# Encoder trunk: GpSimd's adding DMAs and the block sums of seven-block weights held in written order

## The chip, the cores and the metric

The kernel runs on one core of a Trainium2 chip. The metric is the device time of one execution in microseconds, median of three runs. The core has five engines with instruction streams of their own (TensorE, VectorE, ScalarE, GpSimd and SyncE, shown in profiles as PE, DVE, ACT, POOL and SP) and 16 DMA engines. SP issues most of the transfers; POOL issues a few, among them the transfers that add what they fetch to what lies at the destination.

## The reference

Two pre-norm residual layers over 512 tokens of width 1024. The even layer adds two parallel attentions, the odd layer a neighbourhood attention with a learned position bias; each is followed by an MLP, and the MLPs are what the change touches:

```python
def sq_relu_mlp(h, w_up, w_down):        # 1024 -> 4096 -> 1024
    u = jax.nn.relu(h @ w_up)
    return (u * u) @ w_down

def reference(x, norm_mix, ev_w_in, ...):
    h = x
    for layer in range(DEPTH):           # DEPTH = 2
        i = layer // 2
        hn = rmsnorm(h, norm_mix[layer])
        if layer % 2 == 0:
            h = h + hybrid_attention(hn, ev_w_in[i], ...)
        else:
            h = h + neighbourhood_attention(hn, od_w_qkv[i], od_rpb[i], od_w_out[i])
        h = h + sq_relu_mlp(rmsnorm(h, norm_ffn[layer]), ffn_w_up[layer], ffn_w_down[layer])
    return rmsnorm(h, final_norm)
```

All inputs and outputs are float32.

## The kernel before

**Products in three passes.** A float32 operand is split into a high part (`whi`, rounded by ScalarE) and a low part (`wlo`, what is left). A product is three matmuls: high with high, high with low, low with high (`mm3`, L603 to L605).

**Three kinds of weight chunks.** `chunk` loads weights, ScalarE makes the high part (L233) and VectorE subtracts for the low part (L223). `summed_chunk` is for the eight-bank product `product8`: ScalarE writes minus the rounded weights into `wlo` (L255), then POOL issues a DMA that fetches the weights once more and adds them to that (L256); ScalarE makes the high part later (L259). `seven_chunk` is for products after Winograd's variant of Strassen's scheme (seven block products in place of eight): SP loads two blocks of rows (L352), POOL makes four block sums in three instructions (L355 to L357), then ScalarE and VectorE split the seven blocks (L361, L362), and 21 matmuls of 256 columns use them (L447 to L449).

**An MLP.** `first_product` does some of the up projection plainly and the rest in `Seven`; the sums of its activations, in `Seven.sums` (L389, L392, L395), are made by POOL. The down projection has a plain part, then `product8` (eight banks of PSUM at once), and then `Seven` over the rest, 32 chunks of weights in the first MLP. Beside `product8` VectorE and ScalarE turn the remaining activations into sums and parts (`convert`, L389 and L392, L416, L417, L421). In the first MLP alone, SP also writes the bias table of the neighbourhood attention to DRAM at this time (`bias_rows`, 48 small stores `bx<-a`, L1487 to L1493). The last conversions write into slots of SBUF that the bias rows occupy until those stores have been made. After `product8`, VectorE adds its banks to the residual (L1535).

**Order.** `weights(i)` asks for chunk `i`; `begin` and `preload` start later chunks. Outside `fixed_order()` blocks a scheduler orders each engine's instructions by priority and by when it believes them to be ready, so an instruction may stand on its engine earlier or later than it was written. `tc.keep_in_program_order(x)` holds `x` where it was written among the instructions of its engine. Every engine then runs its stream strictly in order. Weight buffers rotate: four of `raw`, three of `whi`, four of `wlo`; `seven_chunk` uses a spare activation slot (`a`) for its weights where enough are free.

Of the kernel before, what the change touches and what calls it, by code (L numbers as in the profile page):

```python
# [12 lines left out]
ALU = mybir.AluOpType  # L13
# [5 lines left out]
P = 128  # L19
# [11 lines left out]
def f32(ap):  # L31
    return ap.bitcast(F32)
# [3 lines left out]
def encoder_kernel(ctx: ExitStack, tc: tile.TileContext, ins, out, dbg=None):  # L36
    nc = tc.nc
    PE, ACT, DVE, POOL, SP = nc.tensor, nc.scalar, nc.vector, nc.gpsimd, nc.sync
# [22 lines left out]
    def nm(s):  # L61
        cnt[0] += 1
        return f"{s}_{cnt[0]}"
# [183 lines left out]
    def summed_chunk(parts, nk, ncol, heads=None, eng=None):  # L247

        raw = wp.tile([P, 1024], F32, tag="raw", bufs=4, name=nm("raw"))
        v = lambda t: t.rearrange("p (k n) -> p k n", k=nk)  # L250
        (o, n, src), = parts
        SP.dma_start(v(raw), src)
        yield
        lo_ = wp.tile([P, 1024], F32R, tag="wlo", bufs=4, name=nm("wlo"))
        ACT.activation(lo_, raw, AF.Copy, scale=-1.0)  # L255
        POOL.dma_start(v(lo_), src, accum_op=ALU.add)  # L256
        yield
        hi = wp.tile([P, 1024], F32R, tag="whi", name=nm("whi"))
        ACT.activation(hi, raw, AF.Copy)  # L259
        yield v(hi), v(lo_), []  # L260

    def rows(w, k0, nk):
        return w[k0 * P : (k0 + nk) * P, :].rearrange("(k p) n -> p k n", p=P)
# [16 lines left out]
    def begin(i):  # L280
        while begun[0] < len(loaded):
            make = asked[begun[0]][0]
            if make is summed_chunk and begun[0] > i + SUM:
                break
            if make in (summed_chunk, seven_chunk):
                next(loaded[begun[0]])
            begun[0] += 1
# [59 lines left out]
    def seven_chunk(w, k0, c0):  # L347


        slot = Slot(F32) if len(free) > reserve[0] else None  # L350
        raw = slot.t if slot else wp.tile([P, 1024], F32, tag="raw", bufs=4, name=nm("raw"))
        SP.dma_start(raw[:, 0:512].rearrange("p (k n) -> p k n", k=2), rows(w, k0, 2)[:, :, c0 : c0 + 256])  # L352
        r = raw.rearrange("p (b n) -> p b n", n=P)
        yield
        POOL.tensor_tensor(r[:, 6], r[:, 0], r[:, 1], op=ALU.subtract)  # L355
        POOL.tensor_tensor(r[:, 4:6], r[:, 2:3].to_broadcast([P, 2, P]), r[:, 0:7:6], op=ALU.add)  # L356
        POOL.tensor_tensor(r[:, 7], r[:, 3], r[:, 5], op=ALU.subtract)  # L357
        yield
        hi = wp.tile([P, 1024], F32R, tag="whi", name=nm("whi"))
        lo = wp.tile([P, 1024], F32R, tag="wlo", bufs=4, name=nm("wlo"))  # L360
        ACT.activation(hi[:, 0:896], raw[:, 128:1024], AF.Copy)  # L361
        DVE.tensor_tensor(lo[:, 0:896], raw[:, 128:1024], f32(hi[:, 0:896]), op=ALU.subtract)  # L362
        if slot:
            slot.free()
        yield hi, lo, []

    class Seven:
# [63 lines left out]
        def plan(self, w, c0, pairs=None):  # L431

            return [plan(w, pairs[kp] if pairs else 2 * kp, c0, make=seven_chunk) for kp in range(self.np)]
# [86 lines left out]
    def product8(w, first, U, evac, eng=None):  # L520


        nk = len(U)
        ids = [plan([(0, D, rows(w, k, 1))], 1, D, None, eng, make=chunk if n < 2 else summed_chunk)
               for n, k in enumerate(first)]

# [1544 lines left out]
```

## Time and profile before

| | |
|---|---|
| median of the runs | 1172.97 us (1172.79 to 1174.08, 3 runs) |
| profiled execution, device time | 1172.19 us |
| its span in the trace | 1170.3 us |
| TensorE busy | 1149.5 us (98%) |
| VectorE, ScalarE, GpSimd busy | 894.0, 668.4, 597.6 us |
| DMA: bytes, mean rate | 134.37 MB, 115 GB/s |

Of the profiled time, 1.9 us lie outside the span. The first MLP's `product8` runs from about 451 to 507 us, its seven-block product from there to about 587 us; the second MLP's `product8` begins at about 1023 us. A row of a timeline gives start, length, engine, line, operation and tile; in brackets stands how long the engine had been idle and what ended that. A row of the chain of waits gives start, length and the engine or transfer that the end of the run goes back to. A row of waits gives the total, the number and the longest. In "DMA share", 1.00 means that all 16 DMA engines are busy.

### The profile page before, as it was taken

The numbers are of one execution on the slowest core, as the hardware profiler recorded it, in microseconds if no ns is written. First come the engines' busy times: TensorE is split into PE (matmuls) and PEld (weight loads), VectorE is DVE, ScalarE is ACT, GpSimd is POOL, SyncE is SP. The second block draws the span as 40 slices with busy tenths as digits, with TensorE's granted clock in tenths as the row PEclk, the third lists the DMA queues.
The fourth block names the chain that finished last, engine by engine and source line by source line (L and its number), as shares of the span: only waits on it lengthen the run. The fifth ranks groups of instructions, "written<-read, shape, count | busy, mean of one in ns | idle before, by whom it ended". The sixth has DMA issues, their size and how long they took to land.

```text
span 1170.3 us, 20576 instructions
## 1 busy us (share of the span) xinstructions
PE 1149.5 (98%) x7348; PEld 1024.3 (88%) x7348; DVE 894.0 (76%) x1544; ACT 668.4 (57%) x1135; POOL 597.6 (51%) x744
## 2 busy tenths in 40 slices
PE   9999999999999999799999999999999999999997
PEld 7787888887899998599987988988888999989996
DVE  7887988888968876677595676767997787698765
ACT  6676876756256658433453555655552666773445
POOL 4456252305788981179802232222377799435960
PEclk9999999999999999899999999999999999999999
DMA  7322314222522327723346564434343233272332
GB/s 233 108 76 67 94 61 130 64 86 98 159 80 84 103 72 194 198 89 98 128 127 158 136 175 132 128 102 135 100 137 115 83 99 100 61 189 76 126 119 72
DMA packets 115478, 134.37 MB, mean 115 GB/s; under 512 B 9667, under 2 KB 96880, under 8 KB 115376
## 3 DMA queue, kind: packets, MB, share of 16 engines
q1 hardware_dynamic: 111024, 120.09, 33.8%
q0 software_dynamic: 4032, 12.60, 5.4%
q8 instruction: 58, 0.95, 0.3%
q10 hardware_dynamic: 320, 0.36, 0.1%
q14 instruction: 44, 0.36, 0.1%
HBM read 110.61 MB, written 6.29 MB: 100 GB/s over the span
## 4 chain that ended last, share of the span: by engine, by line
PE 79%; DVE 6%; POOL 5%; DMA 3%; issue 3%; SPq 2%; ACT 2%; DVEq 0%; POOLq 0%; ACTq 0%
PE mm L603 8%; PE mm L604 8%; PE mm L605 8%; PE s L1127 3%; PE mm L449 3%; PE mm L447 3%; PE mm L448 3%; PE o L1115 3%; PE t L1102 2%; PE t L447 2%; PE t L449 2%; PE t L448 2%; PE s L605 2%; POOL raw L357 2%; PE s L603 2%
## 5 line engine op out<-in xcount | busy, mean ns | idle before, releaser
L603 PE MATMUL mm<-a,whi 128*128 128x512 f32 x428 | 173.9, 407 | 0.2
L362 DVE TENSOR_TENSOR wlo<-a,whi 128x896 fp32r<-128x896 f32 x103 | 128.1, 1247 | 54.6 <-ACT whi L361 54.3
L604 PE MATMUL mm<-a,whi 128*128 128x512 f32 x428 | 168.9, 395 | 0.0
L605 PE MATMUL mm<-a,wlo 128*128 128x512 f32 x428 | 168.9, 396 | 0.0
L361 ACT ACTIVATE whi<-a 128x896 fp32r<-128x896 f32 x103 | 97.8, 949 | 105.3 <-PE o L604 27.5
L233 ACT ACTIVATE whi<-raw 128x1024 fp32r<-128x1024 f32 (+3 forms) x100 | 92.2, 924 | 68.1 <-PE s L604 19.4
L223 DVE TENSOR_TENSOR wlo<-raw,whi 128x1024 fp32r<-128x1024 f32 (+4 forms) x97 | 110.6, 1145 | 24.1 <-ACT whi L233 19.7
L449 PE MATMUL mm<-a,wlo 128*128 128x256 f32 x430 | 120.5, 280 | 1.0 <-DVE wlo L362 1.0
L447 PE MATMUL mm<-a,whi 128*128 128x256 f32 x430 | 120.7, 281 | 0.0
L448 PE MATMUL mm<-a,whi 128*128 128x256 f32 x430 | 120.4, 280 | 0.0
L362 DVE TENSOR_TENSOR wlo<-raw,whi 128x896 fp32r<-128x896 f32 x61 | 73.2, 1203 | 49.7 <-ACT whi L361 49.3
L361 ACT ACTIVATE whi<-raw 128x896 fp32r<-128x896 f32 x61 | 57.9, 953 | 86.4 <-POOL raw L357 54.5
L356 POOL TENSOR_TENSOR a<-a 128x256 f32<-128x256 f32 x103 | 98.6, 957 | 8.0
L355 POOL TENSOR_TENSOR a<-a 128x128 f32<-128x128 f32 x103 | 60.2, 584 | 81.6 <-DMA a<-in_ffn_w_up_dram 75.7
L357 POOL TENSOR_TENSOR a<-a 128x128 f32<-128x128 f32 x103 | 96.5, 937 | 8.0
L605 PEld LDWEIGHTS mm<-a,wlo 128*128 128x128 f32 x428 | 80.3, 188 | 18.4
L603 PEld LDWEIGHTS mm<-a,whi 128*128 128x128 f32 x428 | 80.4, 188 | 17.1 <-issue 1.3
L604 PEld LDWEIGHTS mm<-a,whi 128*128 128x128 f32 x428 | 80.7, 189 | 14.9 <-DVE a L960 0.2
L1714 POOL TENSOR_SCALAR p<-p,ti 128x256 f32<-128x256 f32 x64 | 35.4, 563 | 105.5 <-DVE ti L1713 92.3
L1135 POOL TENSOR_SCALAR p<-p,ti 128x512 f32<-128x512 f32 x64 | 45.4, 710 | 82.9 <-DVE ti L1134 55.1
L447 PE MATMUL t<-a,whi 128*128 128x256 f32 x312 | 87.6, 281 | 0.0
L448 PE MATMUL t<-a,whi 128*128 128x256 f32 x312 | 87.4, 280 | 0.0
(430 smaller groups left out, 3615.6 us busy)
## 6 DMA issues: line engine op xcount, KB each, us to landing
a<-in_ffn_w_up_dram SPq DMA_DIRECT2D x102, 256.0 KB
raw<-in_ffn_w_down_dram SPq DMA_DIRECT2D x34, 512.0 KB
raw<-in_ffn_w_down_dram SPq DMA_DIRECT2D x59, 256.0 KB
raw<-in_od_w_qkv_dram SPq DMA_DIRECT2D x64, 128.0 KB
raw<-in_ffn_w_up_dram SPq DMA_DIRECT2D x12, 512.0 KB
wlo<-in_ffn_w_down_dram POOLq DMA_DIRECT2D x12, 512.0 KB, 7.0
a<-a SPq DMA_DIRECT2D x18, 256.0 KB
bias<-bx SPq DMA_DIRECT2D x16, 256.0 KB
```

Source lines behind the costliest of these rows:

```text
L223: z = lambda: (eng or DVE).tensor_tensor(to, src, f32(high), op=ALU.subtract)
L233: ACT.activation(hi[:, 0:m], raw[:, 0:m], AF.Copy)
L356: POOL.tensor_tensor(r[:, 4:6], r[:, 2:3].to_broadcast([P, 2, P]), r[:, 0:7:6], op=ALU.add)
L357: POOL.tensor_tensor(r[:, 7], r[:, 3], r[:, 5], op=ALU.subtract)
L361: ACT.activation(hi[:, 0:896], raw[:, 128:1024], AF.Copy)
L362: DVE.tensor_tensor(lo[:, 0:896], raw[:, 128:1024], f32(hi[:, 0:896]), op=ALU.subtract)
L447: PE.matmul(o, wh, x[:, 0], start=kp == 0 and n in (0, 1, 3, 5), stop=False, skip_group_check=True)
L448: PE.matmul(o, wh, x[:, 1], start=False, stop=False, skip_group_check=True)
L449: PE.matmul(o, wl, x[:, 0], start=False, stop=kp == self.np - 1, skip_group_check=True)
L603: PE.matmul(o, wh, xh, start=first, stop=False)
L604: PE.matmul(o, wh, xl, start=False, stop=False)
L605: PE.matmul(o, wl, xh, start=False, stop=last)
```

## The change

Two places are wrapped in `tc.keep_in_program_order`: the adding DMA of `summed_chunk`, and the three block sums of `seven_chunk`. No instruction is added, removed or altered, and the orders of PE, DVE, ACT and SP stay as they were; only POOL's order moves. From L355 on, line numbers of the new kernel are one higher.

```diff
@@ summed_chunk
-        POOL.dma_start(v(lo_), src, accum_op=ALU.add)
+        tc.keep_in_program_order(POOL.dma_start(v(lo_), src, accum_op=ALU.add))
@@ seven_chunk
-        POOL.tensor_tensor(r[:, 6], r[:, 0], r[:, 1], op=ALU.subtract)
-        POOL.tensor_tensor(r[:, 4:6], r[:, 2:3].to_broadcast([P, 2, P]), r[:, 0:7:6], op=ALU.add)
-        POOL.tensor_tensor(r[:, 7], r[:, 3], r[:, 5], op=ALU.subtract)
+        held = tc.keep_in_program_order
+        held(POOL.tensor_tensor(r[:, 6], r[:, 0], r[:, 1], op=ALU.subtract))
+        held(POOL.tensor_tensor(r[:, 4:6], r[:, 2:3].to_broadcast([P, 2, P]), r[:, 0:7:6], op=ALU.add))
+        held(POOL.tensor_tensor(r[:, 7], r[:, 3], r[:, 5], op=ALU.subtract))
```

POOL's stream in the first MLP, beside `product8`, before. `wlo_5602` and `wlo_5666` are the low parts of the last two chunks of `product8`; `raw_5600`, `raw_5664` are the weights of the first two chunks of the seven-block product behind it:

```order
L256 DMA wlo_5444<-in_ffn_w_down_dram 128x1024
L256 DMA wlo_5536<-in_ffn_w_down_dram 128x1024
L355 TENSOR_TENSOR raw_5600<-raw_5600 128x128
L356 TENSOR_TENSOR raw_5600<-raw_5600 128x256
L357 TENSOR_TENSOR raw_5600<-raw_5600 128x128
L256 DMA wlo_5602<-in_ffn_w_down_dram 128x1024
L256 DMA wlo_5666<-in_ffn_w_down_dram 128x1024
L355 TENSOR_TENSOR raw_5664<-raw_5664 128x128
```

and now:

```order
L256 DMA wlo_5444<-in_ffn_w_down_dram 128x1024
L256 DMA wlo_5536<-in_ffn_w_down_dram 128x1024
L256 DMA wlo_5602<-in_ffn_w_down_dram 128x1024
L256 DMA wlo_5666<-in_ffn_w_down_dram 128x1024
L356 TENSOR_TENSOR raw_5600<-raw_5600 128x128
L357 TENSOR_TENSOR raw_5600<-raw_5600 128x256
L358 TENSOR_TENSOR raw_5600<-raw_5600 128x128
L356 TENSOR_TENSOR raw_5664<-raw_5664 128x128
```

The two adding DMAs no longer stand behind the first chunk's sums; those sums stand behind both DMAs.

POOL's stream in the second MLP at the same stage, before. `wlo_12000` and `wlo_12046` are again the last two low parts, `raw_11998` and `raw_12044` the first two seven-block chunks; `a_12234` is the sixth, loaded into a spare slot:

```order
L355 TENSOR_TENSOR raw_11998<-raw_11998 128x128
L356 TENSOR_TENSOR raw_11998<-raw_11998 128x256
L357 TENSOR_TENSOR raw_11998<-raw_11998 128x128
L256 DMA wlo_12000<-in_ffn_w_down_dram 128x1024
L355 TENSOR_TENSOR raw_12044<-raw_12044 128x128
L356 TENSOR_TENSOR raw_12044<-raw_12044 128x256
L357 TENSOR_TENSOR raw_12044<-raw_12044 128x128
L256 DMA wlo_12046<-in_ffn_w_down_dram 128x1024
L355 TENSOR_TENSOR raw_12097<-raw_12097 128x128
L355 TENSOR_TENSOR a_12234<-a_12234 128x128
```

and now:

```order
L256 DMA wlo_12000<-in_ffn_w_down_dram 128x1024
L256 DMA wlo_12046<-in_ffn_w_down_dram 128x1024
L356 TENSOR_TENSOR raw_11998<-raw_11998 128x128
L357 TENSOR_TENSOR raw_11998<-raw_11998 128x256
L358 TENSOR_TENSOR raw_11998<-raw_11998 128x128
L356 TENSOR_TENSOR raw_12044<-raw_12044 128x128
L357 TENSOR_TENSOR raw_12044<-raw_12044 128x256
L358 TENSOR_TENSOR raw_12044<-raw_12044 128x128
L356 TENSOR_TENSOR raw_12097<-raw_12097 128x128
```

Here too both DMAs go ahead of the sums, and the sums of `a_12234`, which were interleaved with those of `raw_12097`, go behind two further chunks, to the place after `raw_12161`.

In the up projections the sums move as well. At the start of the first MLP, POOL's stream before; `a_3491` is the second seven-block chunk of weights, and L389 to L395 on `a_3203`, `a_3200` are the first of four sets of activation sums:

```order
L355 TENSOR_TENSOR a_3491<-a_3491 128x128
L356 TENSOR_TENSOR a_3491<-a_3491 128x256
L357 TENSOR_TENSOR a_3491<-a_3491 128x128
L389 TENSOR_TENSOR a_3203<-a_3200 128x512
L392 TENSOR_TENSOR a_3200<-a_3200,a_3203 128x256
L395 TENSOR_TENSOR a_3203<-a_3200 128x256
```

and now, behind the fourth set:

```order
L390 TENSOR_TENSOR a_3334<-a_3331 128x512
L393 TENSOR_TENSOR a_3331<-a_3331,a_3334 128x256
L396 TENSOR_TENSOR a_3334<-a_3331 128x256
L356 TENSOR_TENSOR a_3445<-a_3445 128x128
L357 TENSOR_TENSOR a_3445<-a_3445 128x256
L358 TENSOR_TENSOR a_3445<-a_3445 128x128
L356 TENSOR_TENSOR a_3491<-a_3491 128x128
L357 TENSOR_TENSOR a_3491<-a_3491 128x256
L358 TENSOR_TENSOR a_3491<-a_3491 128x128
```

The first two chunks' sums (`a_3445` stood among the softmax rows of the attention before) come after the activations'. In the same stage one chunk that is loaded early and used late (`raw_5143`) is now summed shortly before its use, and two neighbours (`a_3796`, `a_3826`) change places. The second MLP's up projection changes in the same way.

## The prediction

> **What bounds the kernel now.** I read the chain of waits by engine first, then who TensorE waits for, then the place where it waits.
>
> ```profile
> PE 79%; DVE 6%; POOL 5%; DMA 3%; issue 3%; SPq 2%; ACT 2%; DVEq 0%; POOLq 0%; ACTq 0%
> PE s L605 <- DMA wlo<-in_ffn_w_down_dram: 7.8, 2, 6.1
> PE mm L449 <- DVE wlo L362: 1.0, 1, 1.0
> ```
>
> The first row is the chain, the others TensorE's waits (us, times, longest). TensorE ends the run; of all it waits for, the adding DMAs of `wlo` are the only large item, and the next is 1.0 us. So I look at the timelines of PE, POOL and ACT around that wait, at the end of the first MLP's `product8`.
>
> ```profile
> 484.22 0.39 PE L604 MATMUL s<-p,whi 128*128 128x512 f32 x1
> 490.74 0.79 PE L605 MATMUL s<-p,wlo 128*128 128x512 f32 x1 [6.14 <-DMA wlo<-in_ffn_w_down_dram]
> ...
> 506.44 0.39 PE L605 MATMUL s<-p,wlo 128*128 128x512 f32 x1
> 463.53 0.86 POOL L256 DMA_DIRECT2D wlo<-in_ffn_w_down_dram  x1 [13.83 <-ACT wlo L255]
> 465.52 0.86 POOL L256 DMA_DIRECT2D wlo<-in_ffn_w_down_dram  x1 [1.13 <-DMA bx<-a]
> 481.06 0.45 POOL L355 TENSOR_TENSOR raw<-raw 128x128 f32<-128x128 f32 x1 [14.69 <-ACT a L416]
> 483.22 1.77 POOL L256 DMA_DIRECT2D wlo<-in_ffn_w_down_dram  x2
> 469.06 1.04 ACT L255 ACTIVATE wlo<-raw 128x1024 fp32r<-128x1024 f32 x1
> 476.78 1.06 ACT L255 ACTIVATE wlo<-raw 128x1024 fp32r<-128x1024 f32 x1 [1.77 <-DMA raw<-in_ffn_w_down_dram]
> ```
>
> POOL stood 14.69 us before the sums of `raw_5600`, whose load SP issues late, and the last two adding DMAs stood behind them until 483.22. Their inputs were ready at 469.06 + 1.04 = 470.1 and 476.78 + 1.06 = 477.8 us.
>
> The wait also halved TensorE's clock:
>
> ```profile
> 484.00:494.00 10.00, 2.25 (x6) 1.01 (x4) 2.72 (x6) 0.49 (x1) 0.98 (x2) 0.78 0.96 198
> 488.00:490.00 2.00, 0.00 (x0) 0.00 (x0) 0.00 (x0) 0.00 (x0) 0.00 (x0) 0.90 0.87 161
> 498.00:500.00 2.00, 2.00 (x6) 1.54 (x6) 2.00 (x3) 0.53 (x1) 1.92 (x3) 0.54 0.01 2
> 472.00:484.00 12.00, 12.00 (x54) 9.77 (x53) 9.22 (x16) 6.71 (x11) 2.78 (x5) 1.00 0.61 186
> ```
>
> The last three columns are granted clock, DMA share and GB/s. A mean of 0.90 over 488 to 490 means half speed from 489.6, and 0.54 over 498 to 500 means full speed again from 499.8. TensorE's last matmul had ended at 484.61, 5.0 us before the drop.
>
> But the stall is not what the end goes back to. Here the chain of waits runs past it:
>
> ```profile
> 467.49 9.85 DMA bx<-a
> 485.36 9.56 DMA bx<-a
> 497.87 1.26 DVE wlo L362
> 507.13 1.07 DVE wlo L362
> 508.22 2.62 DMA raw<-in_ffn_w_down_dram
> 510.98 1.35 POOL raw L355
> 569.01 0.96 ACT whi L361
> ```
>
> It follows the stores of the bias table on SP to the last one, which lands at 485.36 + 9.56 = 494.92; then VectorE's work, which could not go on until that store left its slot; the low part of seven-block chunk 1 at 507.13 + 1.07 = 508.20, which frees a buffer; a load of 2.62 us; and then POOL's sums, back to back until 569.
>
> **The change part by part.**
>
> *The two adding DMAs, first MLP.* They can now go out at 470.1 and at about 478 to 480 (the load for the second shares the DMA engines, which I give up to 2 us). The first pair's tempo is the nearest for landing: the pair issued at 483.22 let TensorE start at 490.74, 7.5 us. So 470.1 + 7.5 = 478 and 478 to 480 + 7.5 = 485.5 to 487.5, against 484.61: no wait for the first, 0 to 3 us for the second, 1 taken. TensorE's naive gain is the 7.8 us of waits and half of the 499.8 - 490.7 = 9.1 us at half clock, 4.5, less 1: 11.3 us. `product8` (48 matmuls in its last phase, 46 left after 484.22, each 0.23 us as the last rows show: 506.44 ends it) would end at about 496 rather than 507.
>
> *What is late next.* The seven-block product then waits for chunk 1, ready at 508.20, less what the chain moves. Before, TensorE came to it at 506.7 + 2.5 = 509.2, after it was ready. If the chain did not move, TensorE would merely stand there instead. So the gain is the shift of the last store's landing, and no more.
>
> *How far that shift goes.* A load on quiet queues takes 2.62 us; SP issues a store every 0.61 us when nothing holds it:
>
> ```profile
> 484.75 0.57 SPq L1491 DMA_DIRECT2D bx<-a  x1
> 466.59 0.85 SPq L252 DMA_DIRECT2D raw<-in_ffn_w_down_dram  x1
> 467.49 1.09 SPq L1487 DMA_DIRECT2D bx<-a  x1
> ...
> 476.74 0.38 SPq L352 DMA_DIRECT2D raw<-in_ffn_w_down_dram  x1
> q0 software_dynamic: 288, 1.05, 53.4%
> ```
>
> With nothing beside it the last store would be out at 485.36 + 0.61 and land 2.62 later, at 488.6: 6.3 us is the upper bound. The two DMAs are moved, not removed. The last row (POOL's queue in 483 to 495) says they take 0.534 x 12 = 6.4 us of all 16 engines; between 472 and 484 those stand idle for (1 - 0.61) x 12 = 4.7 us. If the spare time is all used, 6.4 - 4.7 = 1.7 us remains to push the stores, and the shift is 6.3 - 1.7 = 4.6 us. The other estimate is from what the earlier pair did to SP: seven stores from 467.49 to 476.74 took 9.25 us where 7 x 0.61 = 4.3 would do, so 4.9 us were lost. Lost once more, the last store lands at 488.6 + 4.9 = 493.5: 1.4 us. I take the mean, 3.0 us.
>
> The Trainium skill (DMA: Bandwidth & Descriptors, Queues, rings and completion order) says that each DMA engine takes turns between queues packet by packet. By that rule the stores fall behind wherever an adding transfer runs, and the shift would be nearer the smaller estimate, 1.4 us; the long landings at 467.49 and 485.36, both beside such a pair, agree with it.
>
> *Sums of the first down chunk.* `raw_5600` now waits for the DMA of `wlo_5666` (out by 481): its sums go at 481.06 to 481.9, long before VectorE uses them at 497.87. Nothing is lost, and with that DMA 3 us later still nothing.
>
> *Up projections.* The first two chunks' sums go behind the activations'. They fill a gap:
>
> ```profile
> 283.21 1.07 POOL L395 TENSOR_TENSOR a<-a 128x256 f32<-128x256 f32 x1
> 290.38 0.47 POOL L355 TENSOR_TENSOR a<-a 128x128 f32<-128x128 f32 x1 [6.09 <-DMA a<-in_ffn_w_up_dram]
> 310.53 0.95 ACT L361 ACTIVATE whi<-a 128x896 fp32r<-128x896 f32 x1 [4.51 <-PE o L604]
> 429.30 0.46 POOL L355 TENSOR_TENSOR a<-a 128x128 f32<-128x128 f32 x1
> 431.81 0.46 POOL L355 TENSOR_TENSOR a<-a 128x128 f32<-128x128 f32 x1
> 438.93 0.94 ACT L361 ACTIVATE whi<-raw 128x896 fp32r<-128x896 f32 x1
> 443.48 0.94 ACT L361 ACTIVATE whi<-a 128x896 fp32r<-128x896 f32 x1
> ```
>
> Two chunks of 431.81 - 429.30 = 2.5 us each fit into 6.09 us of idleness, and the first is needed at 310.53, over 20 us later. `raw_5143` now comes in before the last two chunks; they end at worst 2.5 us later, at 437, and are used from 438.93 on, the last at 443.48. 0 us, at worst 1 if that cover is gone.
>
> *Second MLP.* Here TensorE had no such wait, so earlier DMAs give nothing.
>
> ```profile
> 1050.58 0.88 POOL L256 DMA_DIRECT2D wlo<-in_ffn_w_down_dram  x1
> 1059.41 0.94 ACT L361 ACTIVATE whi<-raw 128x896 fp32r<-128x896 f32 x1
> 1071.54 1.36 POOL L355 TENSOR_TENSOR raw<-raw 128x128 f32<-128x128 f32 x1 [5.01 <-DMA raw<-in_ffn_w_down_dram]
> 1074.80 0.95 ACT L361 ACTIVATE whi<-a 128x896 fp32r<-128x896 f32 x1 [1.46 <-PE o L448]
> ```
>
> Even if the last DMA went no earlier than 1050.58 + 0.88, the first two chunks' sums behind it end at 1051.5 + 5.0 = 1056.5, before 1059.41; `a_12234` fits into the 5.01 us before 1071.54 and is used at 1074.80. 0 us.
>
> *Sum.* The profiled execution took 1172.19 us (span 1170.3 and 1.9 around it), 0.78 below the median. 1172.19 - 3.0 = 1169.2; on the median, 1172.97 - 3.0 = **1170.0 us**. Behind 510.98 loads, POOL and TensorE move with the chain, so I let the 3.0 us reach the end; a measurement of this kernel tells about 0.2% (2.3 us) from no change.
>
> **The rivals.**
>
> *A new stall halves the clock (same; 25%).* TensorE comes to the seven-block product about 10 us early and stands before chunks 0 and 1. VectorE makes their low parts 507.13 - 497.87 = 9.3 us apart; less 2.5 us of matmuls for chunk 0, up to 6.8 us are idle, broken by two matmuls once chunk 1's high part is there. The drop came 5.0 us after the last matmul, and half speed then cost 4.5 us. By then TensorE is 509.2 - 505.2 = 4 us ahead, so it would come out level, and only what TensorE later waits for falls away: about 1 us, 1172.0. Against it: the two matmuls break the gap into some 3 and 4 us.
>
> The Trainium skill (TensorE: Matmul & The Clock Gate, HAM oscillation — how this bites in real kernels) puts the limit at gaps above about 3.4 us, and its Part 1 lets the clock come back after about as long a time of work; by that the broken gap could halve the clock too, at an estimated 3.4 / 2 = 1.7 us. The trace differs on the second: TensorE worked 9.1 us at half speed. On the first no gap of that length decides here.
>
> *Hidden (same; 10%).* The stores land as late as before, shift 0 to 2 us: 1172.0.
>
> *The whole stall comes back (faster; 6%).* The stores are so much quicker that the low part of chunk 1 no longer holds TensorE: 1172.97 - 11.3 = 1161.7. It would take a shift beyond the bound of 6.3.
>
> *The stores are pushed further back (slower; 17%).* All of SP's stores from 470 on now run beside two adding DMAs in place of none. Lost time on SP decides: above 6.3 us the last store lands after 494.92. If each of the two costs what the earlier pair cost together, 9.8 us are lost; the landing is 488.6 + 9.8 = 498.4, 3.5 us late, and TensorE, idle for over 10 us, restarts at half clock: 1172.97 + 3.5 = 1176.5 us, up to 4.5 more. For it: in the earlier pair's time one store took 9.85 us. Against it: that pair ran beside the load issued at 466.59 as well.
>
> That the DMAs would not move is ruled out by POOL's order; that they wait for something else on POOL belongs to the hidden case.
>
> **How the numbers follow.** The forecast (shift of 2.4 to 6.3 us) has 42%, the rivals 25, 10, 6 and 17. Faster: 42 + 6 = 48%; same: 35%; slower: 17%. The range ends at 1166.0, just under 1172.97 - 6.3 = 1166.7, and at 1176.5, so that the 6% below and about 8% of the slower case are left out. The forecast's own range is 1166.7 to 1170.6.
>
> **What would show it.** In the changed profile: L256 on POOL at about 470 and 479; no wait of 6 us for L605 there; the last `bx` store landing near 492; a wait of TensorE before L447 to L449 in its place, near 500 to 505; POOL's sums going back to back from about 508 rather than 511; the rest of the run moved by the same amount. A last store at 495 or later, or a granted clock of 0.50 beyond 505, would make the prediction wrong.

## The result, and the profile after

| | before | after |
|---|---|---|
| median (runs) | 1173.05 us (12) | 1171.74 us (12; 1170.06 to 1173.27) |
| ratio, 95% interval | | 0.9989, 0.998 to 0.9998 |
| the same pair, measured again | 1173.33 us (15) | 1171.65 us (11): 0.9985, 0.9974 to 0.9996 |
| profiled execution (span) | 1172.19 us (1170.3) | 1171.35 us (1169.6) |

The change gains 1.3 us at the first measurement (0.2 to 2.3 by the interval) and 1.7 at the second. The forecast was 1170.0, a gain of 3.0.

The chain of waits by engine, and whom TensorE waits for (us in all, times, longest), after:

```profile
PE 75%; DVE 7%; POOL 5%; DMA 4%; issue 4%; ACT 2%; SPq 2%; DVEq 0%; POOLq 0%; ACTq 0%
```

```profile
PE s L448 <- DVE hT L1536: 2.4, 1, 2.4
PE s L606 <- DMA wlo<-in_ffn_w_down_dram: 1.4, 1, 1.4
PE s L450 <- DVE wlo L363: 1.4, 3, 0.8
PE mm L450 <- DVE wlo L363: 1.2, 2, 1.1
PE t L448 <- DVE hT L1536: 1.2, 2, 0.6
```

The 7.8 us of waits for the adding DMAs have become 1.4. In their place stands a wait that the kernel before did not have: the first matmuls of the seven-block product wait for VectorE's residual adds (L1536). TensorE's timeline at that place:

```profile
487.92 0.50 PE L606 MATMUL s<-p,wlo 128*128 128x512 f32 x1 [1.43 <-DMA wlo<-in_ffn_w_down_dram]
497.57 0.39 PE L606 MATMUL s<-p,wlo 128*128 128x512 f32 x1
500.39 0.36 PE L448 MATMUL s<-a,whi 128*128 128x256 f32 x1 [2.43 <-DVE hT L1536]
501.57 0.38 PE L448 MATMUL t<-a,whi 128*128 128x256 f32 x1 [0.58 <-DVE hT L1536]
503.38 0.58 PE L448 MATMUL t<-a,whi 128*128 128x256 f32 x1 [0.60 <-DVE hT L1536]
```

`product8` ends at 498 instead of 507 us. Its banks of PSUM (`s`, `t`, `o`) are the ones that the seven-block product writes next, and each is free only when VectorE has added it to the residual. Busy time by engine in windows (the last three columns are granted clock, DMA share, GB/s) shows what that costs:

```profile
498.00:500.00 2.00, 0.00 (x0) 0.00 (x0) 2.00 (x4) 0.00 (x0) 1.84 (x4) 1.00 0.29 77
502.00:504.00 2.00, 1.40 (x8) 1.11 (x7) 2.00 (x3) 2.00 (x3) 1.84 (x4) 0.53 0.00 0
506.00:508.00 2.00, 1.87 (x9) 1.58 (x8) 2.00 (x4) 0.95 (x1) 0.00 (x0) 0.50 0.00 0
```

From 498 to 500 TensorE does nothing while VectorE (third figure) is busy throughout; from 502 to 508 TensorE runs at half clock. VectorE is late because it and ScalarE stood for the stores (the experiments below take that wait away). The rows of POOL, SP, ACT, DVE and POOL again, in order of time:

```profile
471.74 0.86 POOL L256 DMA_DIRECT2D wlo<-in_ffn_w_down_dram  x1 [4.02 <-ACT wlo L255]
480.99 0.86 POOL L256 DMA_DIRECT2D wlo<-in_ffn_w_down_dram  x1 [8.39 <-DMA bx<-a]
490.71 0.57 SPq L1494 DMA_DIRECT2D bx<-a  x1
493.29 0.63 ACT L417 ACTIVATE a<-sc 128x512 fp32r<-128x512 f32 x1 [6.75 <-DMA bx<-a]
499.57 0.67 DVE L1536 TENSOR_TENSOR hT<-hT,s 128x512 f32<-128x512 f32 x1
506.11 1.08 DVE L363 TENSOR_TENSOR wlo<-raw,whi 128x896 fp32r<-128x896 f32 x1
510.07 1.25 POOL L356 TENSOR_TENSOR raw<-raw 128x128 f32<-128x128 f32 x1 [5.35 <-DVE wlo L363]
```

The adding DMAs go out at 471.74 and 480.99. SP's last store is issued 5.35 us later than before (490.71, before 485.36); those transfers now run beside the stores. The landings behind it are short: the first of ScalarE's conversions that write into the stores' slots starts at 493.29, and SP, which waits for all the stores before it loads the table, goes on at 494.08. The same two rows before, and then SP's row after:

```profile
494.27 0.63 ACT L416 ACTIVATE a<-sc 128x512 fp32r<-128x512 f32 x1 [9.78 <-DMA bx<-a]
495.04 0.89 SPq L1788 DMA_DIRECT2D bias<-bx  x2
```

```profile
494.08 0.88 SPq L1789 DMA_DIRECT2D bias<-bx  x2
```

So the stores are out of the way 1.0 us earlier. The low part of chunk 1 is ready at 507.19 instead of 508.20, and POOL's sums go back to back from 510.07 instead of 510.98. In this pair of traces the span is 0.7 us shorter.

TensorE's own position is the clearest measure. The next table gives, for each trace of this study but the two of the failed try, how much later (+) or earlier (-) the same matmul starts than in the first trace of the kernel before: the median over the matmuls within 3 us of the time named (times as in that first trace). The kernels are those of the experiments below; "pins" are the added `keep_in_program_order`, "rows" those of the bias table.

| us, at | 362 | 410 | 440 | 540 | 930 | 1080 |
|---|---|---|---|---|---|---|
| before, second trace | 0.34 | 0.66 | 0.66 | -0.41 | 0.41 | 1.03 |
| pins in the up projections | 1.00 | 1.78 | 1.78 | 0.96 | 0.90 | 3.54 |
| after | 0.29 | 1.20 | 1.20 | -1.28 | -1.25 | -0.76 |
| after, second trace | 0.61 | 1.47 | 1.47 | -3.20 | -2.85 | -0.46 |
| pins in the down projections | 0.64 | 0.90 | 0.90 | -3.69 | -3.32 | -3.12 |
| pins in the first down projection | 0.07 | 0.32 | 0.32 | -2.97 | -2.95 | -1.12 |
| rows in own tiles, after | 0.24 | 1.21 | 1.32 | -3.87 | -4.92 | -3.67 |
| rows in own tiles, before | -0.26 | -0.23 | -0.12 | -0.43 | -1.47 | -0.58 |
| rows in own tiles, pins in the down projections | 0.14 | 0.19 | 0.29 | -6.78 | -7.34 | -6.77 |
| rows beside the seven-block product | -0.05 | 0.77 | 0.87 | -9.81 | -10.17 | -7.94 |

In the changed kernel TensorE loses 0.9 us between 362 and 410 us, in the first up projection, and gains 2.5 us between 440 and 540 us. The loss sits at two matmuls that wait for a low part of seven-block weights; the larger, before and after:

```profile
396.46 0.39 PE L449 MATMUL s<-a,wlo 128*128 128x256 f32 x1 [0.16 <-DVE wlo L362]
```

```profile
397.67 0.38 PE L450 MATMUL s<-a,wlo 128*128 128x256 f32 x1 [0.76 <-DVE wlo L363]
```

### The profile page after: what moved, and what is told of

It reads as the page before. It is cut to its first block, busy times and chain, and to the rows that moved or that the text cites. A ratio compares the mean times of both kernels' runs of the same rounds, so it can differ in the third digit from the quotient of the medians.

```text
span 1169.6 us, 20581 instructions
## 1 busy us (share of the span) xinstructions
PE 1150.6 (98%) x7348; PEld 1025.9 (88%) x7348; DVE 892.6 (76%) x1544; ACT 668.4 (57%) x1135; POOL 602.0 (51%) x744
## 4 chain that ended last, share of the span: by engine, by line
PE 75%; DVE 7%; POOL 5%; DMA 4%; issue 4%; ACT 2%; SPq 2%; DVEq 0%; POOLq 0%; ACTq 0%
PE mm L604 8%; PE mm L605 8%; PE mm L606 8%; PE s L1128 3%; PE mm L450 3%; PE mm L448 3%; PE mm L449 3%; PE o L1116 3%; PE t L1103 2%; PE s L606 2%; PE s L604 2%; POOL raw L358 2%; PE s L605 2%; PE t L448 2%; PE t L450 2%
## 5 line engine op out<-in xcount | busy, mean ns | idle before, releaser
L358 POOL TENSOR_TENSOR a<-a 128x128 f32<-128x128 f32 x103 | 98.5, 956 | 8.1
L357 POOL TENSOR_TENSOR a<-a 128x256 f32<-128x256 f32 x103 | 94.9, 921 | 8.1
L450 PE MATMUL t<-a,wlo 128*128 128x256 f32 x312 | 88.0, 282 | 0.0
```

Source lines behind the costliest of these rows:

```text
L357: held(POOL.tensor_tensor(r[:, 4:6], r[:, 2:3].to_broadcast([P, 2, P]), r[:, 0:7:6], op=ALU.add))
L358: held(POOL.tensor_tensor(r[:, 7], r[:, 3], r[:, 5], op=ALU.subtract))
L450: PE.matmul(o, wl, x[:, 0], start=False, stop=kp == self.np - 1, skip_group_check=True)
```

## The experiments

My theory after the two traces (A): the two adding DMAs bring a gain, bounded by the landing of the last store; the block sums in the up projections lose part of it. Rivals: the loss in the up projection is scatter (B); VectorE has that much work left whatever the stores do (C).

**Which pins do what.** Pinning the adding DMAs alone leaves all five streams as they were before; pinning the sums alone makes all of the change. So the split is by projection, with the sums:

```diff
-        held = tc.keep_in_program_order
+        held = tc.keep_in_program_order if w.shape[0] > D else lambda z: z
```

> The pins act in the down projections alone: the up projections' streams are those of the kernel before, the down projections' those of the changed one. Theory A (the traces' difference is real: the pins won about 2.5 us in the first down projection and lost about 1.2 us in the first up projection): TensorE runs level with the kernel before, within 0.3 us, until 440 us, is about 2.5 us ahead behind the first MLP's product8, and the time is 1170.0 to 1170.8, over 1 us below the changed kernel. Rival B (the 1.2 us lost in the up projection are the scatter of one execution): the time is that of the changed kernel, 1171.7, and the up projection may be late here too.

With the condition reversed (`== D`) and no pin on the DMAs:

> The pins act in the up projections alone; the first product8 has the stream of the kernel before. Theory A: TensorE is late by 0.9 to 1.3 us at 440 us, stands 6 and 1.7 us for the adding DMAs as in the kernel before, and the time is 1174.0 to 1174.5. Rival B: the time is that of the kernel before, 1173.0, and TensorE is level with it at 440 us.

Down projections alone: 1171.65 us against 1173.0, ratio 0.9986 (0.9977 to 0.9994). Up projections alone: 1173.74, ratio 1.0 (0.9991 to 1.0008). So the gain comes from the down projections. That the up projections' pins cost something is not seen in the times; the place in the trace shows it, with 0.8 us lost between 362 and 410 us (0.9 in the changed kernel), and 0.3 us where they are absent. TensorE stands for the adding DMAs as before:

```profile
491.59 0.80 PE L606 MATMUL s<-p,wlo 128*128 128x512 f32 x1 [5.21 <-DMA wlo<-in_ffn_w_down_dram]
495.13 0.80 PE L606 MATMUL s<-p,wlo 128*128 128x512 f32 x1 [1.89 <-DMA wlo<-in_ffn_w_down_dram]
```

Theory A's time for the down projections alone, over 1 us below the changed kernel, did not come, and for the up projections alone the time lies between the two theories'.

**The two DMAs alone.** The smallest form of the change, with the pins tied to one set of weights:

```diff
+            pinned[0] = w                      # in mlp, for l == 0, w = ffn_w_down[0]
-        held = tc.keep_in_program_order
+        held = tc.keep_in_program_order if w is pinned[0] else lambda z: z
```

> The block sums pinned in the first MLP's down projection alone: against the kernel before, GpSimd's stream differs only in the two adding DMAs that go ahead of the first chunk's three sums. Theory A (the whole gain comes from these two DMAs, the rest of the change gives nothing or loses): the same as the kernel with both down projections pinned, 1170.5 to 1172 against 1173.0 to 1173.7 for the kernel before; in the trace TensorE is level with the kernel before at 440 us within 0.4 us and 2 to 4.5 us ahead of it at 540 us. Rival: the second MLP's new order takes part, and this kernel gains under 0.5 us.

1172.09 against 1173.69 us: ratio 0.9986 (0.9977 to 0.9994), the same as with both down projections. Moving two DMAs ahead of three sums is worth 1.6 us, between 0.7 and 2.7; no gain of the rest of the change is seen beside that.

**Fewer stores beside `product8`, a failed try.** Sixteen of the 48 stores write a constant; here they go out before the first MLP from a scratch tile:

```diff
+    def neg_rows():                              # called before the first stage of the first MLP
+        t = scratch()
+        POOL.memset(t[:, 0:128], NEG)
+        ...  SP.dma_start(bxv[1, c][:, :, 128 - 128 * v : 256 - 128 * v], t[:, 0:128])
-            SP.dma_start(bxv[1, c][:, :, 128 - 128 * v : 256 - 128 * v], Fe.t[:, 256:384])
```

> The changed kernel with the 16 stores that fill the masked halves of the bias table (a constant) issued from a small constant tile before the first MLP, so that 32 of SP's 48 stores are left beside product8. Theory A (the stores set when VectorE and then TensorE go on): the last store is issued some 16 x 0.61 = 9.8 us earlier, near 481, VectorE's idle 4.5 us before its last conversions go, TensorE no longer waits for banks of the residual adds, and the time falls by 3 to 6 us below the changed kernel, 1166 to 1169. Rival C (VectorE's own queue of conversions and adds is the limit, stores or not): the time stays within 1.5 us of the changed kernel, 1170.2 or more, and TensorE waits for the residual adds as long as before (2.4 us).

> The kernel before, without pins, with the same 16 constant stores issued early. The scheduler, left free, puts one adding DMA behind the sums of the first seven-block chunk and one behind those of the second. Theory A (the early stores free the end of product8, and then the wait for the adding DMAs decides): TensorE still stands 3 to 9 us for the adding DMAs and the time is 2 to 6 us above that of the changed kernel with early constants. Rival D (with the stores out of the way POOL's order no longer matters): the two are within 1 us of each other.

Both came out slower: 1178.49 us, ratio 1.0039 (1.0026 to 1.0051), and 1175.98, ratio 1.0025 (1.0015 to 1.0035). No theory had that. TensorE's largest wait, and the chain of waits, in the first of the two:

```profile
PE s L604 <- ACT whi L259: 5.3, 2, 3.4
```

```profile
474.23 6.86 DMA bx<-a
481.34 0.70 ACT a L417 x2
482.04 0.95 ACT whi L259
```

The last store is issued at 474.23, earlier than I expected. But ScalarE's order is another: conversions into the slots now stand ahead of high parts that TensorE needs, presumably since the scheduler expects the slots free earlier, too. ScalarE then stands for the store until 481, and TensorE with it. The run says that the stores hold whatever stands behind them; as ScalarE's order moved with it, it doesn't say what fewer stores are worth.

**No conversion waits for the stores.** The rows are stored from the tile `rb`, idle at that time, and a small new one, instead of two slots. The stores keep their number and place, for which those of the constant are held:

```diff
-        R, Fi, Fe = Slot(F32), Slot(F32), Slot(F32)
+        R, Fi, Fe = Slot(F32), keep([P, S], F32, "rb"), keep([P, 376], F32, "rows_e")
...
-            SP.dma_start(bxv[1, c][:, :, 128 - 128 * v : 256 - 128 * v], Fe.t[:, 256:384])
+            held(SP.dma_start(bxv[1, c][:, :, 128 - 128 * v : 256 - 128 * v], Fe[:, 248:376]))
```

> The changed kernel, but the bias table's rows are stored from tiles of their own (one idle tile and one small new one) instead of two of the slots that the last conversions write into, so that no conversion has to wait for SP's stores; the stores themselves, their number and their place among SP's transfers stay. Theory A (the landing of the last store holds VectorE, and VectorE holds TensorE and GpSimd's sums): VectorE's idle time of 4.5 us and ScalarE's of 6.8 us before 494 us go, GpSimd's sums go back to back some 3 to 5 us earlier, TensorE's wait for the residual adds falls below 1 us, and the time is 1166 to 1169, 3 to 5 us below the changed kernel. Rival C (VectorE has that much left to do anyway): the time stays within 1.5 us of the changed kernel, 1170.2 or more.

> The kernel before with the same tiles of their own for the bias rows; GpSimd's order around the adding DMAs is that of the kernel before (two of them behind the first chunk's sums). Theory A: TensorE still stands 6 to 8 us for the adding DMAs and halves its clock, so the gain is at most what TensorE waited for behind it (about 1 us): 1172 to 1173.5; the pins are then worth 4 to 6 us rather than 1.3. Rival C: both kernels stay where they were, the pins worth 1 to 2 us.

1167.76 us with the pins, ratio 0.9949 (0.9934 to 0.9964) to the kernel before at 1173.74; 1172.12 without, ratio 0.9987 (0.9979 to 0.9995). The pins are now worth 4.4 us. Theory A's times came in both, and C falls. (Besides the tiles, a few of ScalarE's conversions and high parts, one of SP's transfers and GpSimd's filling of the rows stand in other places than before; for ScalarE and SP these are the same with pins and without, and VectorE's order is that of the kernel before, so the 4.4 us are the pins' own; what the tiles alone bring can't be told apart from these moves.) With pins, TensorE no longer waits for the residual adds; VectorE starts the first at 494.95 instead of 499.57, and the fifth at 499.96:

```profile
494.95 0.68 DVE L1536 TENSOR_TENSOR hT<-hT,s 128x512 f32<-128x512 f32 x1
499.96 0.68 DVE L1536 TENSOR_TENSOR hT<-hT,mm 128x512 f32<-128x512 f32 x1
```

What remains is the adding DMA itself, with pins and without:

```profile
489.96 0.79 PE L606 MATMUL s<-p,wlo 128*128 128x512 f32 x1 [3.06 <-DMA wlo<-in_ffn_w_down_dram]
```

```profile
490.34 0.80 PE L605 MATMUL s<-p,wlo 128*128 128x512 f32 x1 [5.71 <-DMA wlo<-in_ffn_w_down_dram]
493.92 0.79 PE L605 MATMUL s<-p,wlo 128*128 128x512 f32 x1 [1.93 <-DMA wlo<-in_ffn_w_down_dram]
```

**The faster versions.** First the same tiles with pins in the down projections alone; then, in addition, the stores beside the seven-block product instead of `product8`:

```diff
+                if i < 15: next(bias, None)      # beside product8: the loads and the first store
-            next(bias, None)
-            next(bias, None)
...
             for i, _ in enumerate(u7.run(ids[m], evac)):
                 beside(m, i)
+                if i % 3 == 2: next(bias, None)
```

> The changed kernel with tiles of their own for the bias rows and the block sums pinned in the down projections alone. If the up projection's pins cost about 1 us in each MLP, as two traces with them and two without show, this is 0.7 to 2 us below the kernel with all pins and the same tiles, 1165 to 1168, and the fastest of all; if those losses are scatter, it is level with it.

> As the kernel with tiles of their own for the bias rows and pins in the down projections, but 47 of SP's 48 stores go beside the seven-block product instead of beside product8 (all in written order). Theory A (the stores and the adding DMAs delay each other): with no stores beside them the last adding DMA lands in time, TensorE's remaining wait for it (2.5 us) and the half clock behind it (about 3 us at half speed, 1.5 us lost) go, and the time is 1162.5 to 1164.5, 1.5 to 3 us below that kernel's 1165.8. Rival: the adding DMA is slow by itself, or the stores now hold the loads of the seven-block weights behind them on SP: the same time or up to 3 us more.

1165.82 us, ratio 0.9943 (0.9926 to 0.996), 1.9 us below the same tiles with all pins by the medians and 0.7 by the ratios, with intervals that overlap, so it isn't shown which of its two forecasts came; and 1163.09 us against 1173.69, ratio 0.9908 (0.9893 to 0.9923), 10.6 us below the kernel before. In the second, TensorE's waits hold neither the adding DMAs nor the residual adds:

```profile
PE s L450 <- DVE wlo L363: 2.4, 4, 1.2
PE o L157 <- POOL zeros L130: 1.0, 1, 1.0
```

Busy time by engine in windows of the same kernel (TensorE first, granted clock third from the end):

```profile
484.00:494.00 10.00, 10.00 (x46) 8.29 (x45) 9.86 (x17) 3.38 (x7) 3.07 (x5) 1.00 0.09 28
494.00:502.00 8.00, 7.87 (x55) 7.07 (x55) 8.00 (x12) 3.80 (x5) 2.61 (x4) 1.00 0.17 51
```

It is busy almost throughout at full clock, and between 440 and 540 us it gains 10.7 us. Beside `product8` the adding DMAs now land sooner; their number, size and median time from issue to landing between 440 and 500 us, with the stores beside them (pins in the down projections, own tiles) and without:

```profile
wlo<-in_ffn_w_down_dram POOLq DMA_DIRECT2D x6, 512.0 KB, 8.1
```

```profile
wlo<-in_ffn_w_down_dram POOLq DMA_DIRECT2D x6, 512.0 KB, 6.2
```

So theory A came, in time and in mechanism. What the stores' new place is worth without the pins was not measured.

**Second traces.**

> The changed kernel once more, for a second trace and more times. If what the first trace showed is steady: TensorE loses 0.8 to 1.0 us between 362 and 410 us (up projection, pins), gains 2.5 to 4.5 us between 440 and 540, the loss in the second up projection is anything from 0.2 to 2.6, and the time is 1.0 to 1.8 us below that of the kernel before. If the up projection's loss was scatter it is under 0.4 us here.

> The kernel before once more, for a second trace. If the first trace was a lucky execution in the second MLP's up projection, as the ten other traces suggest (0.2 to 2.6 us lost there against it, 1.3 on average), this one loses 0.5 to 2.5 us there; between 440 and 540 us it is level with the first trace within 0.8 us. If instead the second up projection is slower for the pins alone, it is level there.

After: 1171.65 us, ratio 0.9985 (0.9974 to 0.9996); before, one run, 1173.17. The table has both. The loss between 362 and 410 us is 0.91, 0.86 and 0.78 us in the three traces with these pins and the up projection otherwise unchanged, and 0.32, 0.26 and 0.25 in the three further traces without them, beside 0 in the first: on average 0.6 us more, and steady, so B falls there; that this reaches the end isn't shown. (In other versions it is 0.8 us without these pins, with the rows beside the seven-block product, and 0.1 us with them, with the early constants; so it hangs on more than the pins.) In the second MLP, between 930 and 1080 us, the loss is 0.49, 2.39 and 2.64 us with the pins, 0.62, 0.20 and 1.83 without: 1.2 us more on average, but within scatter.

## Why the prediction was right and where it was wrong

The measured 1171.7 lies in the stated range, 1166.0 to 1176.5, but outside the forecast's own, 1166.7 to 1170.6. The chain that bounds the gain was named rightly, and GpSimd's sums moved by 2.5 us on average (0.9 in the first trace) where 3.0 was forecast. The time gained is less, 1.3 to 1.7 us, and that it comes out nearest to two rivals, at 1172.0, is in good part chance.

- *The adding DMAs.* Forecast for about 470 and 479 us; less TensorE's 1.2 us of delay, they went at 470.5 and 479.8. The wait for the second, 0 to 3 us with 1 taken, was 1.43 in the first trace. The naive gain of 11.3 us is about what TensorE gained where nothing took it back (10.7 us, rows beside the seven-block product).
- *What is late next.* The cause was right, VectorE's work behind the last store, but not the first instruction: TensorE met the banks that the residual adds still held, at 500.39, before it came to chunk 1. Then it came to chunk 1 just in time, as forecast: its first matmul with that low part starts at 507.25, 0.06 us after the part is ready (507.19), and as close behind it in the three other traces with these two DMAs early and the rows in slots. In the kernel before it started 1.2 us after that part was ready.
- *The clock.* I counted it against the rival that two matmuls break the gap. Gaps of 2.43, 0.58 and 0.60 us halved the clock all the same, for 6.8 us, and it halved at this place in the three other traces with these two DMAs early and the rows in slots. Half speed lasted until 508.95, beyond the 505 us that I had named as a sign of being wrong. Against its position at 440 us TensorE's lead over the kernel before fell from 10.0 us (at the matmul that starts there at 499.8) to 2.5 (at 510.5). But the half clock did not set the time. The seven-block product ends with a wait for a low part, before and after:

```profile
575.14 0.38 PE L449 MATMUL mm<-a,wlo 128*128 128x256 f32 x1 [0.95 <-DVE wlo L362]
```

```profile
574.12 0.38 PE L450 MATMUL mm<-a,wlo 128*128 128x256 f32 x1 [1.06 <-DVE wlo L363]
```

In all seven traces with the rows in slots (the failed try's apart) this matmul starts 64.05 to 64.29 us after the first of GpSimd's back-to-back sums (510.98 and 510.07 here), with 0.95 to 1.06 us of waiting before it. So the sums decide when TensorE gets through, as forecast, and what the half clock cost TensorE it would otherwise have waited. The rival's half clock came; that the time is near its 1172.0 is not its doing.

- *The shift of the stores, 3.0 us.* Its parts held: the stores were pushed back, and the gain stayed far below the stall. Where SP goes on behind the stores, the four traces with the two DMAs early and rows in slots have 494.08, 493.23, 492.34 and 492.81 against 495.04 and 495.00 in the two of before: a shift of 0.9 to 2.7 us, 1.9 on average. That is nearer to the smaller of my two estimates, 1.4 us, which the Trainium skill's rule favoured (DMA: Bandwidth & Descriptors, Queues, rings and completion order: turns packet by packet), and the first trace alone would belong to the rival "hidden". GpSimd's sums go back to back at 510.07, 508.45, 507.55 and 508.02 against 510.98 and 511.04, 2.5 us earlier on average; why by more than the stores isn't settled. Between 440 and 540 us TensorE gains 2.48, 4.67, 4.59 and 3.29 us in the four traces, 3.8 on average, against 0, 1.07 and 0.82 in the three without: a difference of 3.1 us. (These gains hold what TensorE had lost up to 440 us and got back, as the sums decide.)
- *"0 us, at worst 1 if that cover is gone" for the up projections* is a step that failed by size: 0.6 us in the first. I had checked the first chunks and the last, not the ones between: GpSimd's sums run almost back to back there, and a new order among them shows up as waits for low parts at 367 and 397 us (the second is there without the pins too, but shorter).
- *"I let the 3.0 us reach the end"* is the other. With only the two DMAs moved, the time falls by 1.6 us (0.7 to 2.7), half of the 3.1 in the traces. Part of it is that traces are single executions: the first of before is 0.86 us below its kernel's median, and the second ends 1.1 us later in span; that of the pins in the down projections is the fastest of its 11 runs, and that of the pins in the up projections the slowest of its 11. What takes the rest isn't settled: the second up projection varies by 2 us between executions, and one or two traces for each kernel can't say whether that is chance.
- *The second MLP* gives nothing by the times of the kernel without it (0.9986 with and without), as forecast.

The rival "pushed further back" didn't come: the last store was issued 5.35 us later, but it landed within 3.4 us (SP went on at 494.08), where its landing had taken 9.56; no adding DMA was issued in the 9.7 us before it.

## What to carry to other kernels

When a stall ends, ask what the freed engine meets next, which buffers (here PSUM banks) it needs and who frees them: the end of a stall of 7.8 us was worth 1.6 us while the stores held slots that the conversions wanted, 4.4 us when they did not, and with the stores moved out of that stage as well the whole came to 10.6 us. Shared slots make an unimportant transfer critical. A wait that stands at the same place in every version, before and after, shows what decides there, and what is lost ahead of it (here half clock) may cost nothing. And a pin that is meant for one place also holds everywhere else that the same helper runs, so narrow it.

## What the hardware showed that I had not expected

The half clock comes in steps. By the granted clock it lasted 10.2 us in both traces of before (489.6 to 499.8 in the first, with the second wait of 1.70 us in it), 6.8 us after (502.1 to 508.9) and 3.4 us in the second trace of after (501.8 to 505.3). With rows in own tiles a gap of 3.06 us brought 6.8 us, and one of 2.52 us (with pins in the down projections alone) 3.4 us, here in three windows around it:

```profile
486.00:488.00 2.00, 0.00 (x0) 0.00 (x0) 1.97 (x5) 0.63 (x1) 0.65 (x1) 1.00 0.53 146
490.00:492.00 2.00, 2.00 (x6) 1.54 (x6) 2.00 (x4) 1.47 (x3) 0.00 (x0) 0.50 0.51 152
492.00:494.00 2.00, 2.00 (x9) 1.62 (x8) 2.00 (x5) 0.00 (x0) 0.00 (x0) 0.82 0.96 294
```

So a gap of 2.5 us was enough, while the one of 1.43 us at 487.92 in the first trace of after left the clock at 1.00. The price was one, two or three times 3.4 us at half speed. The Trainium skill (TensorE: Matmul & The Clock Gate, Part 1) describes a free-running window of about 3.4 us, which these lengths agree with; its rule of thumb, gaps above 3.4 us (HAM oscillation — how this bites in real kernels), does not hold here.
